# A two-layer decoder trunk: the attention's head pairs as one pipeline, with 64-row scores and w_o's first two groups by turns

## The chip, the core and the metric

The kernel runs on one NeuronCore of a Trainium2 chip: TensorE (PE, with its weight loads PEld), VectorE (DVE), ScalarE (ACT), GpSimd (POOL) and SyncE (SP), each with its own queue of instructions, joined by semaphores. The metric is the device time of one launch in microseconds (us).

## What is computed

One sequence of 256 positions, width 2048, two layers: a recurrent layer (RG-LRU) with a SwiGLU FFN, then a shared K/V projection, an attention layer and a second FFN. The change is in the attention layer only:

```python
D_MODEL = 2048; SEQ = 256; HEAD_DIM = 64; N_HEADS = 32; N_KV_HEADS = 4; WINDOW = BLOCK = 128
...
def attn_block(x, g, w_q, q_g, sinks, w_o, k_band, v_band):
    h = rms_norm(x, g)
    q = rms_norm((h @ w_q).reshape(bsz, s, N_KV_HEADS, GROUP, HEAD_DIM), q_g)
    ...
    scores = jnp.einsum("bnqhgd,bnkhd->bnhgqk", q, k_band) * (1.0 / math.sqrt(HEAD_DIM))
    scores = jnp.where(mask, scores, NEG_INF)
    ...                                   # one learned sink logit per head joins the softmax
    probs = jax.nn.softmax(jnp.concatenate([scores, sink], axis=-1), axis=-1)[..., :-1]
    out = jnp.einsum("bnhgqk,bnkhd->bnqhgd", probs, v_band)
    return x + out.reshape(bsz, s, N_HEADS * HEAD_DIM) @ w_o
```

Queries of block 0 see the 128 keys of their own block, queries of block 1 the 256 keys of both.

## The kernel before

Features lie on the 128 partitions and the 256 positions (`T`) along the free dimension. Every big product is a sum of three: weights and activations are split into a rounded high part and a rest (`hi`, `lo` of the weights; the two halves of a slot `s` of the activations), and high x high, high x rest and rest x high are added in PSUM. `group` makes one group of 512 output features: four PSUM banks, one for each tile `f` of 128 features, and `nk // 2` steps (jobs) of two input tiles each. Each step is one 512 KB weight load on SP's queue, one split on ACT (L242) and DVE (L243), and 24 matmuls of 256 columns at L280. In the steps that `SYNC` names, (0, 2, 5), three times two of them are merged to one of 512 columns ("h" in `products`), in a row. Such a bank then holds two halves, which the drain adds (`two`).

`stream` runs all steps in order. Attention, norms and splits of activations are background tasks (generators), stepped once or more at each half step (`half_tick`, `run_bg`), where their matmuls are put between the products. Counters of estimated DVE and ACT time (`self.dve`, `self.act`, `pe`) limit how many steps are taken. Tile's scheduler then sets the final order on each engine's queue, and may put a background matmul some rows later than the code has it. At most `MISC` = 4 of the 8 banks are lent to background tasks.

Attention has 16 pairs of heads (128 features each). Each group of w_q brings four pairs and a task that computes their norm (L910) and starts one `head_pair` per pair. A pair's four stages:

- scores (L799 to L801): K stands in `kd`, two slots (high and rest), each with the head's 64 features on partitions 0 to 63 for the first head and 64 to 127 for the second, zeros elsewhere, so that one matmul over 128 rows gives both heads: for block 0 three of 256 columns, for block 1 three of 512;
- softmax on DVE (L813 adds the mask and takes the maximum, then `ts`) and ACT (Exp);
- transposes (L847), six of 128 x 128, three to a bank, which ACT copies to two slots;
- values (L866 to L868): per head three fp32 matmuls of 64 output rows, the two heads in the two column halves of the array; then the split to `at[k]`, an input tile of w_o.

Pairs run beside each other as far as banks and slots allow. `project` with w_o has four groups of eight steps, in each of which step c waits for `at[2c]` and `at[2c+1]`; `residual` adds the result to x and prepares the next norm.

Of the kernel before, what the change touches and what calls it, by code (L numbers as in the profile page):

```python
# [48 lines left out]
class Trunk:  # L49
# [5 lines left out]
    NORM = 6  # L55
    MISC = 4
# [215 lines left out]
    def products(self, todo, ps, hi, lo, x2, begun, last):  # L272


        for n, (k, f, p) in enumerate(todo):
            if 2 * n in (len(todo), len(todo) + 1):
                self.half_tick()
            high, c0, c1 = self.PARTS[p]
            w = (hi if high else lo)[:, k * 512 + f * P:k * 512 + f * P + P]
            self.nc.tensor.matmul(ps[f][:, 0:c1 - c0], w, x2[k][:, c0:c1], start=f not in begun,  # L280
                                  stop=last and all(q[1] != f for q in todo[n + 1:]))
            begun.add(f)

    def group(self, src, nk, xs, done, last=False, sync=()):


        st = {}
        both = [(k, f) for k in range(2) for f in range(4)]
        for c in range(nk // 2):
            def mm(hi, lo, c=c):  # L290
                if c == 0:
                    st["ps"] = [self.bank() for _ in range(4)]
# [15 lines left out]
                self.products(todo, st["ps"], hi, lo, x2, st["begun"], c == nk // 2 - 1)  # L308
                if last:
                    for q in x2:  # L310
                        self.free(q)
                if c == nk // 2 - 1:
                    done([(p, bool(sync) and f < 2) for f, p in enumerate(st["ps"])])
            self.jobs.append((src(c), mm))

    def pull(self, bank, o=None, r=None):

        ps, two = bank
# [11 lines left out]
        self.free_bank(ps)  # L330
        return o
# [65 lines left out]
    def residual(self, g, ps, gains, r, out=None):  # L397
        for f in range(4):
            xt = self.x[g][:, f, :]
            p, two = ps[f]  # L400
# [5 lines left out]
            self.free_bank(p)  # L406
            if out is not None:
                self.nc.sync.dma_start(out[:, 4 * g + f, :], xt)
# [10 lines left out]
    def project(self, w, nk, xs, gains, r, out=None):  # L419
        for g in range(4):  # L420
            def done(ps, g=g):
                self.residual(g, ps, gains, r, out)
            self.group(lambda c, g=g: w[g, c], nk, xs, done, g == 3, () if out is not None and g == 3 else self.SYNC)
# [233 lines left out]
    def kv(self, xs, r, gains):  # L657
# [7 lines left out]
        def done(ps):  # L665
            k0 = [self.pull((p, False)) for p in ps[:2]]
# [4 lines left out]
            def task():  # L671
# [31 lines left out]
                for h in range(4):  # L703
# [21 lines left out]
        for c in range(8):  # L725
            def mm(hi, lo, c=c):
                if c == 0:
# [3 lines left out]
                    for h in range(4):  # L731
                        self.kd[h].ap = [self.slot() for _ in range(2)]
                        self.kvs += self.kd[h].ap
                        for q in self.kd[h].ap:
                            self.dve += 280
                            nc.vector.memset(q[0:64, T:2 * T].bitcast(F32), 0.0)
                            nc.vector.memset(q[64:P, 0:T].bitcast(F32), 0.0)
# [35 lines left out]
    def attn(self, xs, r, gains, rn):  # L773
# [4 lines left out]
        self.pairs = 0  # L778
# [4 lines left out]
        def head_pair(k, qs, rr):  # L783

            while not (self.kd[k // 4].ready and self.v[0].ready and self.v[1].ready):
                yield 1
            kd, f = self.kd[k // 4].ap, k % 4
            sm = self.half()
            mx, nm, es, den = (sm[:, 4 * i:4 * i + 4] for i in range(4))
            ps, sc = [], []  # L790
            for b in range(2):
                while not self.room():
                    yield 1
                p = self.mbank()
                n = P * (b + 1)
                o = p[:, 0:2 * n].rearrange("p (h n) -> p h n", h=2)
                kh, kl = (q.rearrange("p (h n) -> p h n", h=2)[:, :, 0:n] for q in kd)
                qh, ql = (qs[:, i * T + b * P:i * T + b * P + P] for i in range(2))
                nc.tensor.matmul(o, qh, kh, start=True, stop=False)  # L799
                nc.tensor.matmul(o, qh, kl, start=False, stop=False)  # L800
                nc.tensor.matmul(o, ql, kh, start=False, stop=True)  # L801
                ps.append(p)
                self.pe(330 * (b + 1))
            yield 1
            for hh in range(2):
                while not self.slots:
                    yield 1
                s = self.slot(F32)
                sc.append(s)
                for b, c0, c1 in blocks:  # L810
# [3 lines left out]
                        s[:, c0:c1], ps[b][:, hh * (c1 - c0):(hh + 1) * (c1 - c0)], con[:, K_MASK + c0:K_MASK + c1],  # L814
                        rr[:, b * 8 + f * 2 + hh:b * 8 + f * 2 + hh + 1],
                        par[:, C_SINK + 4 * k + hh:C_SINK + 4 * k + hh + 1], ALU.add, ALU.max,
                        accum_out=mx[:, i:i + 1])
                yield
            for p in ps:
                self.free_mbank(p)  # L820
            self.free(qs)
# [18 lines left out]
            yield 1  # L840
            ps, pT = [], []
            for hh in range(2):
                while not self.room():
                    yield 1
                p = self.mbank()
                for j in range(3):
                    nc.tensor.transpose(p[:, j * P:(j + 1) * P], sc[hh][:, j * P:(j + 1) * P], one)  # L847
                ps.append(p)
                self.pe(400)
            yield 1  # L850
            for hh in range(2):
                s = self.slot(F32)
                pT.append(s)
                self.a(s[:, 0:384], ps[hh][:, 0:384])
                self.free_mbank(ps[hh])
                self.free(sc[hh])
                yield
            yield 1
            while not self.room():
                yield 1  # L860
            p = self.mbank()
            c = (k // 4) * HD
            v0, v1 = (q.ap[:, c:c + HD] for q in self.v)
            for hh in range(2):
                o, t = p[64 * hh:64 * hh + 64, :], pT[hh]
                nc.tensor.matmul(o[:, 0:P], v0, t[:, 0:P], start=True, stop=True)  # L866
                nc.tensor.matmul(o[:, P:T], v0, t[:, P:T], start=True, stop=False)  # L867
                nc.tensor.matmul(o[:, P:T], v1, t[:, T:3 * P], start=False, stop=True)  # L868
                self.free(t)
                self.pe(400)  # L870
            yield 1
            s = self.slot()
            self.split_act(s, p[:, 0:T])
            self.free_mbank(p)
            at[k].ap = s
            at[k].ready = True
            self.pairs += 1
            if self.pairs == ND:
                for q in self.kvs:
                    self.free(q)  # L880
            yield

        for g in range(4):
            def done(ps, g=g):
# [6 lines left out]
                def task():  # L891
# [21 lines left out]
                    rr, m, t = (self.rrs[g % 2][:, 16 * i:16 * i + 16] for i in range(3))  # L913
# [11 lines left out]
                    for f in range(4):  # L925
                        self.spawn(head_pair(4 * g + f, qs[f], rr))
                        yield 2
                self.spawn(task())
            self.group(lambda c, g=g: w[g, c], ND, xs, done, g == 3, self.SYNC)
        self.project(self.d["w_o"], ND, at, gains, rn)  # L930


    def run(self):
# [5 lines left out]
        self.rrs = [const.tile([P, 48], F32, name=f"rr{i}") for i in range(2)]  # L939
# [85 lines left out]
```

## Time and profile before

| | before |
|---|---|
| median of 3 runs | 1997.57 us (1997.15 to 2000.5) |
| profiled execution, device time | 1996.68 us |
| its span in the trace | 1994.9 us |
| TensorE clock granted | 1.00 |
| q1 (all weight loads) | 373.60 MB, 58.3% of 16 DMA engines |

A row of the timeline has start, length, engine, line, operation, out<-in, rows*columns of the array in use, the moving operand's size and the count of instructions merged in it. In `out<-in` the moving operand comes first, then the weights: `b` is a PSUM bank, `s` a slot, `con` constants. The ends of matmuls are modelled, so the distance of two starts tells what one costs. An fp32 matmul appears as two instructions. In the rows of windows come the busy times of PE, PEld, DVE, ACT and POOL, then the clock, DMA's share and GB/s.

### The profile page before, as it was taken

How to read it: one execution, taken by the hardware profiler on the slowest of the kernel's cores; microseconds unless marked ns; L12 is line 12 of the kernel's file. 1: busy time of each engine (PE TensorE's matmuls, PEld its weight loads, DVE VectorE, ACT ScalarE, POOL GpSimd, SP SyncE). 2: the span in 40 equal slices, each digit the busy share in tenths (PEclk: the TensorE clock that was granted, in tenths of full speed). 3: DMA queues.
4: the chain of work that ended last, by engine and by line, in shares of the span. 5: the costliest groups of instructions: out<-in, count | busy, mean ns of one | idle time of the engine just before them, and what ended most of it. 6: DMA issues, size and time to landing. Idle time of an engine off the chain costs nothing.

```text
span 1994.9 us, 40283 instructions
## 1 busy us (share of the span) xinstructions
PE 1986.6 (100%) x16793; PEld 1953.1 (98%) x16793; DVE 1283.6 (64%) x2067; ACT 1079.3 (54%) x1627; POOL 0.2 (0%) x4
## 2 busy tenths in 40 slices
PE   9999999999999999999999999999999999999999
PEld 8999999999999999999999999999999999999999
DVE  8989866556556655545768786765565566554543
ACT  7798755445445444444556775554454454444342
POOL 0000000000000000000000000000000000000000
PEclk9999999999999999999999999999999999999999
DMA  7655655665666655565654335666666656656664
GB/s 267 201 183 173 216 191 192 197 194 191 196 195 191 197 194 192 194 197 191 194 187 146 119 117 169 192 190 194 197 191 193 196 192 193 197 192 204 206 204 128
DMA packets 105015, 376.58 MB, mean 189 GB/s; under 512 B 11648, under 2 KB 13824, under 8 KB 104832
## 3 DMA queue, kind: packets, MB, share of 16 engines
q1 hardware_dynamic: 104544, 373.60, 58.3%
q8 instruction: 131, 2.15, 0.4%
q14 instruction: 52, 0.43, 0.1%
q10 hardware_dynamic: 288, 0.40, 0.1%
HBM read 371.86 MB, written 2.10 MB: 187 GB/s over the span
## 4 chain that ended last, share of the span: by engine, by line
PE 98%; ACT 1%; DMA 0%; DVE 0%; issue 0%; SPq 0%; DVEq 0%; ACTq 0%
PE b L280 93%; PE b L559 1%; PE b L847 1%; PE b L755 1%; DMA x<-in_x 0%; PE b L910 0%; PE b L866 0%; PE b L799 0%; PE b L801 0%; PE b L800 0%; PE b L868 0%; PE b L867 0%; ACT hi L242 0%; PE b L764 0%; PE b L765 0%
## 5 line engine op out<-in xcount | busy, mean ns | idle before, releaser
L280 PE MATMUL b<-s,hi 128*128 128x256 f32 (+1 forms) x10406 | 1427.0, 283 | 3.7 <-ACT s L106 1.8
L280 PEld LDWEIGHTS b<-s,hi 128*128 128x128 f32 x10406 | 1318.7, 188 | 31.8 <-ACT hi L242 2.5
L243 DVE TENSOR_TENSOR lo<-raw,hi 128x1024 fp32r<-128x1024 f32 (+1 forms) x705 | 860.9, 1222 | 660.7 <-ACT hi L242 657.0
L242 ACT ACTIVATE hi<-raw 128x1024 fp32r<-128x1024 f32 (+1 forms) x705 | 745.7, 1059 | 770.4 <-PE b L280 740.9
L280 PE MATMUL b<-s,lo 128*128 128x256 f32 x5504 | 823.0, 277 | 0.0
L280 PEld LDWEIGHTS b<-s,lo 128*128 128x128 f32 x5504 | 715.1, 188 | 0.0
L106 ACT ACTIVATE t<-b 128x256 f32<-128x256 f32 x134 | 50.4, 385 | 62.2 <-PE b L280 37.8
L106 ACT ACTIVATE h<-h 128x256 f32<-128x256 f32 (+1 forms) x104 | 38.9, 376 | 21.0 <-DVE h L115 21.0
L106 ACT ACTIVATE s<-h 128x256 fp32r<-128x256 f32 (+1 forms) x106 | 42.7, 412 | 12.3 <-DVE h L115 9.8
L106 ACT ACTIVATE s<-s 128x256 f32<-128x256 f32 (+1 forms) x112 | 41.2, 415 | 5.1 <-DVE s L119 4.6
L115 DVE TENSOR_TENSOR h<-b,rstd 128x256 f32<-128x256 f32 x100 | 41.0, 416 | 0.0
L106 ACT ACT_TABLE_LOAD x31 | 39.8, 1283 | 0.5
L115 DVE TENSOR_TENSOR h<-h,rstd 128x256 f32<-128x256 f32 x94 | 39.1, 420 | 1.5
L106 ACT ACTIVATE s<-x,par 128x256 fp32r<-128x256 f32 x80 | 37.9, 498 | 2.6 <-DVE x L115 1.8
L115 DVE TENSOR_TENSOR h<-b,t 128x256 f32<-128x256 f32 x92 | 38.2, 418 | 0.0
L115 DVE TENSOR_TENSOR s<-s,s 128x256 fp32r<-128x256 f32 (+1 forms) x80 | 31.2, 420 | 9.6 <-ACT s L106 9.5
L119 DVE SCALAR_TENSOR_TENSOR s<-x,par,s 128x256 fp32r<-128x256 f32 x80 | 36.7, 479 | 0.5 <-ACT s L106 0.5
L115 DVE TENSOR_TENSOR s<-h,s 128x256 fp32r<-128x256 f32 x88 | 36.6, 418 | 0.0
L115 DVE TENSOR_TENSOR h<-h,h 128x256 f32<-128x256 f32 x88 | 36.5, 416 | 0.0
L106 ACT ACTIVATE s<-b 128x384 f32<-128x384 f32 (+3 forms) x68 | 28.0, 431 | 10.2 <-PE b L868 5.6
L106 ACT ACTIVATE s<-s,h 128x128 f32<-128x128 f32 x64 | 28.3, 444 | 6.2 <-DVE h L124 6.2
L115 DVE TENSOR_TENSOR x<-x,b 128x256 f32<-128x256 f32 x64 | 25.2, 415 | 8.9 <-PE b L280 8.9
(103 smaller groups left out, 618.8 us busy)
## 6 DMA issues: line engine op xcount, KB each, us to landing
raw<-in_ffn_in SPq DMA_DIRECT2D x352, 512.0 KB, 3.9
raw<-in_ffn_out SPq DMA_DIRECT2D x176, 512.0 KB, 3.5
raw<-in_lru_in SPq DMA_DIRECT2D x63, 512.0 KB, 4.0
raw<-in_lru_out SPq DMA_DIRECT2D x32, 512.0 KB, 3.4
raw<-in_w_q SPq DMA_DIRECT2D x32, 512.0 KB, 3.4
raw<-in_w_o SPq DMA_DIRECT2D x32, 512.0 KB, 3.7
raw<-in_gate SPq DMA_DIRECT2D x8, 512.0 KB, 3.7
raw<-in_kv SPq DMA_DIRECT2D x8, 512.0 KB, 3.3
```

The source lines that it names most:

```text
L106: self.nc.scalar.activation(out, in_, func, **kw)
L115: self.nc.vector.tensor_tensor(out, a, b, op)
L119: self.nc.vector.scalar_tensor_tensor(out, a, s, b, op0, op1)
L242: self.nc.scalar.activation(hi[:, q], raw[:, q], AF.Copy)
L243: self.nc.vector.tensor_tensor(lo[:, q], raw[:, q], hi[:, q].bitcast(F32), ALU.subtract)
L280: self.nc.tensor.matmul(ps[f][:, 0:c1 - c0], w, x2[k][:, c0:c1], start=f not in begun, stop=last and all(q[1] != f for q in todo[n + 1:]))
L559: nc.tensor.matmul(out[j], (hi if high else lo)[:, c:c + P], x2[kt][:, q:q + T], start=kt == 0 and high > q, stop=kt == 1 and not high)
L755: nc.tensor.matmul(ps[f][:, 0:T], w0, x2[kt][:, q:q + T], start=k0 + kt == 0 and high > q, stop=k0 + kt == ND - 1 and not high)
L847: nc.tensor.transpose(p[:, j * P:(j + 1) * P], sc[hh][:, j * P:(j + 1) * P], one)
```

## The change

`head_pair` is replaced by one task, `pairs`, that visits three pairs at a time: the values of the oldest, the transposes of the next and the scores of a new one are issued together, then the copies and the softmax. Visits are at least `VISIT` = 3 half steps apart. `kd` becomes one slot per head group, with K in both partition halves and without zeros; each head's scores are matmuls over 64 rows (partitions 0 to 63, or 64 to 127), into a bank of its own. The transposes fill one and a half banks instead of two, and the values use the free half. The values of a head are one matmul of 256 columns and one of 128 instead of three of 128, and the two heads alternate.

w_o's first two groups keep two tiles in a bank (`paired`), two banks each, without the merged 512-column products, and their steps go by turns: six of the first, six of the second, two of the first, two of the second.

```diff
+    VISIT = 3
...
-    def group(self, src, nk, xs, done, last=False, sync=()):
+    def group(self, src, nk, xs, done, last=False, sync=(), paired=False, jobs=None):
...
+                    if paired:
+                        ps = [self.bank() for _ in range(2)]
+                        st["ps"] = [(ps[f // 2][:, f % 2 * T:f % 2 * T + T], False, f // 2, f % 2) for f in range(4)]
+                        st["bank"] = ps
...
-    def project(self, w, nk, xs, gains, r, out=None):
+    def project(self, w, nk, xs, gains, r, out=None, late=0):
+        first = [[], []]
...
+            if late and g < 2:
+                self.group(src, nk, xs, done, paired=True, jobs=first[g])
+                if g:
+                    n = nk // 2 - late
+                    self.jobs += first[0][:n] + first[1][:n] + first[0][n:] + first[1][n:]
...
-                    kh, kl = self.kd[h].ap
-                    for i in range(2):
-                        q, c = slice(64 * i, 64 * i + 64), slice(i * T, i * T + T)
-                        self.a(kh[q, c], p[q, 0:T])
-                        self.tt(kl[q, c], p[q, 0:T], kh[q, c].bitcast(F32), ALU.subtract)
+                    self.split_act(self.kd[h].ap, p[:, 0:T])
...
+        def values(k, pT, p):
+            c = (k // 4) * HD
+            v0, v1 = (q.ap[:, c:c + HD] for q in self.v)
+            o = [p[HD * hh:HD * hh + HD, T:2 * T] for hh in range(2)]
+            for hh in range(2):
+                nc.tensor.matmul(o[hh], v0, pT[0][:, hh * T:(hh + 1) * T], start=True, stop=False)
+            for hh in range(2):
+                nc.tensor.matmul(o[hh][:, P:T], v1, pT[1][:, hh * P:(hh + 1) * P], start=False, stop=True)
...
+        def transposes(sc, ps):
+            for hh in (1, 0):
+                for j in (2, 1, 0):
+                    o = ps[0][:, hh * T + j * P:hh * T + j * P + P] if j < 2 else ps[1][:, hh * P:hh * P + P]
+                    nc.tensor.transpose(o, sc[hh][:, j * P:(j + 1) * P], one)
...
+        def scores(k, qs, ps):
+            kd = self.kd[k // 4].ap
+            for b, c0, c1 in blocks:
+                for i, j in ((1, 0), (0, 0), (0, 1)):
+                    for hh in range(2):
+                        q = slice(HD * hh, HD * hh + HD)
+                        nc.tensor.matmul(ps[hh][:, c0:c1], qs[q, i * T + b * P:i * T + b * P + P],
+                                         kd[q, j * T:j * T + c1 - c0], start=i == 1, stop=j == 1)
...
+        def pairs():
+            A = B = None
...
+                if A:
+                    values(A[0], A[1], pt[1])
+                    self.pe(900)
+                if B:
+                    transposes(B[1], pt)
+                    self.pe(700)
+                if new:
+                    scores(new[0], new[1], ps)
+                    self.pe(900)
+                yield 1
...                      # ACT copies B's transposes, splits A's values; then the new pair's softmax
+                yield max(1, at_tick + self.VISIT - self.tick)
...
-        self.project(self.d["w_o"], ND, at, gains, rn)
+        self.project(self.d["w_o"], ND, at, gains, rn, late=2)
```

PE's queue at the third pair's scores, before (matmuls by line, tile and size; 799 to 801 scores, 847 transposes of the next older pair, 866 to 868 values, 280 products):

```order
L799 MATMUL b_84<-s_11066,s_11676 128x256
L800 MATMUL b_84<-s_11067,s_11676 128x256
L801 MATMUL b_84<-s_11066,s_11676 128x256
L847 MATMUL b_89<-con,s_11840 128x128
L799 MATMUL b_88<-s_11066,s_11676 128x512
L847 MATMUL b_89<-con,s_11840 128x128 x2
L847 MATMUL b_87<-con,s_11843 128x128 x3
L800 MATMUL b_88<-s_11067,s_11676 128x512
L801 MATMUL b_88<-s_11066,s_11676 128x512
L280 MATMUL b_83<-s_11303,lo_80 128x256
L866 MATMUL b_89<-s_11871,s_11090 64x128
L867 MATMUL b_89<-s_11871,s_11090 64x128
```

The same visit now (804 and 806 values, 825 scores, 814 transposes, 281 products; the second and third pair of score rows, which read like the first, are left out):

```order
L804 MATMUL b_83<-s_11811,s_11072 64x256 x2
L806 MATMUL b_83<-s_11812,s_11072 64x128 x2
L825 MATMUL b_88<-s_11068,s_11649 128x128
L825 MATMUL b_89<-s_11068,s_11649 128x128
...
L825 MATMUL b_88<-s_11068,s_11649 128x256
L814 MATMUL b_83<-con,s_11816 128x128
L814 MATMUL b_86<-con,s_11816 128x128 x2
L814 MATMUL b_83<-con,s_11815 128x128
L814 MATMUL b_86<-con,s_11815 128x128 x2
L825 MATMUL b_89<-s_11068,s_11649 128x256
L825 MATMUL b_88<-s_11068,s_11649 128x256
L281 MATMUL b_85<-s_11243,hi_76 128x256 x2
```

The values moved ahead of the scores, the scores alternate between two banks, and the transposes, written ahead of the scores in `pairs`, stand behind the ninth of the twelve.

PE's queue where w_o's first group ends and the next begins, before (`b_83`, `b_87`, `b_85`: banks of the next group):

```order
L280 MATMUL b_88<-s_13307,lo_82 128x256
L280 MATMUL b_88<-s_13323,hi_78 128x256 x2
L280 MATMUL b_88<-s_13323,lo_82 128x256
L280 MATMUL b_83<-s_11967,hi_75 128x512
L280 MATMUL b_83<-s_11970,hi_75 128x512
L280 MATMUL b_87<-s_11967,hi_75 128x512
```

The place behind the last pair's values now (`b_84` and `b_86` the second group's banks, `b_85` and `b_90` the first's):

```order
L804 MATMUL b_87<-s_13452,s_11072 64x256 x2
L806 MATMUL b_87<-s_13453,s_11072 64x128 x2
L281 MATMUL b_86<-s_13067,hi_78 128x256 x4
L281 MATMUL b_84<-s_13003,lo_82 128x256 x2
...
L281 MATMUL b_85<-s_13291,hi_75 128x256 x4
L281 MATMUL b_90<-s_13291,hi_75 128x256 x4
```

Here the sixth step of the second group is followed by the seventh of the first, all in products of 256 columns; the first merged products of 512 columns stand where the third group begins.

More of the change, by code (lines that the diff above doesn't have):

```diff
@@ L270, with products @@
     PARTS = {"h": (1, 0, 2 * T), "a": (1, 0, T), "b": (1, T, 2 * T), "l": (0, 0, T)}
-    def products(self, todo, ps, hi, lo, x2, begun, last):
+    def products(self, todo, ps, hi, lo, x2, begun, last, paired=False):
         for n, (k, f, p) in enumerate(todo):
@@ L279, in products @@
             w = (hi if high else lo)[:, k * 512 + f * P:k * 512 + f * P + P]
-            self.nc.tensor.matmul(ps[f][:, 0:c1 - c0], w, x2[k][:, c0:c1], start=f not in begun,
-                                  stop=last and all(q[1] != f for q in todo[n + 1:]))
-            begun.add(f)
-    def group(self, src, nk, xs, done, last=False, sync=()):
+            self.nc.tensor.matmul(ps[f][0][:, 0:c1 - c0], w, x2[k][:, c0:c1], start=ps[f][2] not in begun,
+                                  stop=last and all(q[1] != f for q in todo[n + 1:]),
+                                  skip_group_check=paired)
+            begun.add(ps[f][2])
+    def group(self, src, nk, xs, done, last=False, sync=(), paired=False, jobs=None):
         st = {}
+        jobs = self.jobs if jobs is None else jobs
         both = [(k, f) for k in range(2) for f in range(4)]
@@ L731, in mm @@
                     for h in range(4):
[L732 to L737, printed above, removed]
+                        self.kd[h].ap = self.slot()
+                        self.kvs.append(self.kd[h].ap)
                     s = self.slot(F32)
@@ L777, in attn @@
         r2 = self.r2
-        self.pairs = 0
         one = con[:, K_ID:K_ID + P]
         blocks = ((0, 0, P), (1, P, 3 * P))
[L783 to L787, printed above, removed]
+        todo = deque()
+        def values(k, pT, p):
[6 more added lines that the diff above has]
+                nc.tensor.matmul(o[hh][:, P:T], v1, pT[1][:, hh * P:(hh + 1) * P], start=False, stop=True)
+            for q in pT:
+                self.free(q)
@@ L788, in head_pair, with softmax @@
+        def softmax(k, rr, ps, sc):
+            f = k % 4
             sm = self.half()
             mx, nm, es, den = (sm[:, 4 * i:4 * i + 4] for i in range(4))
[L790 to L803, printed above, removed]
@@ L858, in head_pair @@
-            yield 1
-            while not self.room():
-                yield 1
[L861 to L881, printed above, removed]
+        def pairs():
+            A = B = None
+            n = 0
+            while n < ND or A or B:
+                new = None
+                if todo and self.kd[todo[0][0] // 4].ready and self.v[0].ready and self.v[1].ready:
+                    new = todo.popleft()
+                    n += 1
+                elif not (A or B):
+                    yield 1
+                    continue
+                at_tick = self.tick
+                count = 2 * bool(A or B) + 2 * bool(new)
+                while self.misc + count > self.MISC or len(self.banks) < count or len(self.slots) < 5:
+                    yield 1
+                pt = [self.mbank() for _ in range(2)] if A or B else None
+                ps = [self.mbank() for _ in range(2)] if new else None
+                if A:
[7 more added lines that the diff above has]
+                    self.pe(900)
+                yield 1
+                nextA = None
+                if B:
+                    s = [self.slot(F32) for _ in range(2)]
+                    self.a(s[0], pt[0])
+                    self.a(s[1][:, 0:T], pt[1][:, 0:T])
+                    nextA = (B[0], s)
+                    yield
+                if A:
+                    s = self.slot()
+                    self.split_act(s, pt[1][:, T:2 * T])
+                    at[A[0]].ap = s
+                    at[A[0]].ready = True
+                    yield
+                for p in pt or ():
+                    self.free_mbank(p)
+                A, B = nextA, None
+                if new:
+                    sc = [self.slot(F32) for _ in range(2)]
+                    yield from softmax(new[0], new[2], ps, sc)
+                    B = (new[0], sc)
+                yield max(1, at_tick + self.VISIT - self.tick)
+            for q in self.kvs:
+                self.free(q)
@@ L938, in run @@
         self.r2 = const.tile([P, 2], F32, name="r2")
-        self.rrs = [const.tile([P, 48], F32, name=f"rr{i}") for i in range(2)]
+        self.rrs = [const.tile([P, 48], F32, name=f"rr{i}") for i in range(4)]
         self.rv = {i: Val() for i in range(4)}
```

66 lines of the change are left out of this document (27 added, 39 removed).

## The prediction

> **What bounds the kernel now.** I read the page first: span, busy shares, the chain that ended last.
>
> ```profile
> span 1994.9 us, 40283 instructions
> PE 1986.6 (100%) x16793; PEld 1953.1 (98%) x16793; DVE 1283.6 (64%) x2067; ACT 1079.3 (54%) x1627; POOL 0.2 (0%) x4
> PE 98%; ACT 1%; DMA 0%; DVE 0%; issue 0%; SPq 0%; DVEq 0%; ACTq 0%
> ```
>
> TensorE carries 98% of the chain. The waits of PE over the whole run are the second view (us in total, times, longest):
>
> ```profile
> PE b L280 <- ACT s L106: 1.8, 1, 1.8
> PE b L280 <- ACT hi L242: 1.8, 2, 1.5
> PE b L251 <- DVE lo L248: 1.2, 1, 1.2
> PE b L384 <- DVE acc L115: 0.4, 1, 0.4
> ```
>
> That is 5.2 us in all, and the same view cut to 1062 to 1225 us, where the attention runs, has no row for PE. So nothing can be won there by shorter waits. The time is what TensorE issues, at the spacing of its matmuls. Third, two stages side by side (PE, PEld, DVE, ACT busy, clock, DMA):
>
> ```profile
> 800.00:1000.00 200.00, 200.00 (x1740) 198.89 (x1738) 111.87 (x139) 93.35 (x116) 0.00 (x0) 1.00 0.59 194
> 1062.00:1203.00 141.00, 141.00 (x1169) 133.04 (x1168) 111.21 (x370) 108.49 (x287) 0.00 (x0) 1.00 0.37 120
> ```
>
> In the attention stage DMA moves 120 GB/s against 194: the weights wait for TensorE. DVE is busy 79% there, ACT 77%; neither ends the chain. Clock 1.00 in both. So the sum below counts starts of matmuls in PE's timeline (start, length, engine, line). "Busy" is no use, since ends overlap.
>
> **Spacing of the big matmuls.** A 256-column product has two paces:
>
> ```profile
> 603.78 1.07 PE L280 MATMUL b<-s,lo 128*128 128x256 f32 x8
> 604.69 1.52 PE L280 MATMUL b<-s,hi 128*128 128x256 f32 x12
> ...
> 1207.74 1.10 PE L280 MATMUL b<-s,lo 128*128 128x256 f32 x8
> 1208.68 2.05 PE L280 MATMUL b<-s,hi 128*128 128x256 f32 x16
> ...
> 1219.98 2.00 PE L280 MATMUL b<-s,hi 128*128 128x256 f32 x13
> 1221.83 1.07 PE L280 MATMUL b<-s,lo 128*128 128x256 f32 x8
> 1222.73 1.52 PE L280 MATMUL b<-s,hi 128*128 128x256 f32 x12
> ```
>
> 0.91/8 = 0.113 us in the long stages, 0.94/8 = 0.1175 after a disturbance. The step back to 0.113 comes at 1219.98, in the row of 13 which holds the three 512-column "h" products of `SYNC`.
>
> **Scores.** One pair before, six matmuls, three of 256 and three of 512 columns:
>
> ```profile
> 1073.93 0.28 PE L799 MATMUL b<-s,s 128*128 128x256 f32 x1
> ...
> 1074.75 0.39 PE L801 MATMUL b<-s,s 128*128 128x512 f32 x1
> 1074.98 2.05 PE L280 MATMUL b<-s,hi 128*128 128x256 f32 x16
> ```
>
> 1.05 us a pair, 16.8 us for 16, and no loss at either edge. The change makes 12 of them, six on rows 0 to 63 and six on rows 64 to 127, three of 128 and three of 256 columns on each. What one costs is not in this trace; the nearest rows bound it. From below: sixteen matmuls with 128 weight columns that move 2 columns each,
>
> ```profile
> 1070.96 1.84 PE L910 MATMUL b<-con,s 128*128 128x2 f32 x16
> 1072.67 0.48 PE L280 MATMUL b<-s,hi 128*128 128x256 f32 x2
> ```
>
> take 1.71 us, 0.107 each: loading 128 weight columns sets that, however little moves. So a half-array score with 128 weight columns is not below 0.107, and I take 0.117 for 128 and 256 columns alike (the row of the same number format). If the two halves run beside each other a pair takes 6 x 0.117 = 0.70, in all 11.2: a gain of 5.6 us. If they run one after the other it is 1.40, a loss of 5.6.
> The Trainium skill (TensorE: Matmul & The Clock Gate, "LDWEIGHTS (loading the stationary operand)") says that the load goes by columns and not by rows; by that half the rows save no load time, and the 0.107 agrees for whole rows. By that rule the sum stands as below; if half the rows loaded in half the time, the three narrow scores could take 0.06 and the sum would be 16 x 3 x 0.057 = 2.7 us lower.
>
> **Values.** One pair before, between big products:
>
> ```profile
> 1098.03 1.80 PE L280 MATMUL b<-s,hi 128*128 128x512 f32 x11
> 1099.76 0.43 PE L866 MATMUL b<-s,s 128*64 128x128 f32 x2
> 1100.03 0.27 PE L867 MATMUL b<-s,s 128*64 128x128 f32 x1
> 1100.03 0.32 PE L866 MATMUL b<-s,s 128*64 128x128 f32 x1
> ...
> 1100.52 0.38 PE L868 MATMUL b<-s,s 128*64 128x128 f32 x2
> 1100.83 0.50 PE L280 MATMUL b<-s,hi 128*128 128x256 f32 x2
> 1101.18 1.10 PE L280 MATMUL b<-s,lo 128*128 128x256 f32 x8
> ```
>
> Each fp32 matmul is two passes (12 rows for 6 in the code), 0.11 apart within a head; the second head's first pass (the second 1100.03) starts when the first head is at its third. The two 64-column halves of the array therefore do run together, the second 0.27 us late. The block reaches from 1099.68 (8 products of 256 and 3 of 512 columns after 1098.03 at 0.1175 and 0.235) to 1101.18 - 2 x 0.1175 = 1100.945: 1.27 us. In it the first pass starts 0.08 late and takes 0.16, not 0.11: 0.14 to enter. From the last pass's end (1100.63 + 0.11) to 1100.945 is 0.20 to leave. Work: 0.93. Two pairs back to back:
>
> ```profile
> 1086.72 0.28 PE L280 MATMUL b<-s,lo 128*128 128x256 f32 x1
> 1086.92 0.43 PE L866 MATMUL b<-s,s 128*64 128x128 f32 x2
> ...
> 1088.34 0.38 PE L868 MATMUL b<-s,s 128*64 128x128 f32 x2
> 1088.65 0.39 PE L799 MATMUL b<-s,s 128*128 128x256 f32 x1
> 1088.88 0.28 PE L800 MATMUL b<-s,s 128*128 128x256 f32 x1
> ```
>
> From 1086.84 to 1088.88 - 0.12 = 1088.76: 1.92, less 0.34 for the edges 1.58. In PE's order of before, counted over the program, there are four such doubles and eight singles: work 4 x 1.58 + 8 x 0.93 = 13.8 us. After the change the heads alternate (`values`), so both start at once: per head two passes of 256 and two of 128 columns, 6 x 0.109 = 0.65; 16 x 0.65 = 10.4. Gain 3.4 us.
>
> **Transposes** are the same 96, 0.109 apart, and only the edge differs:
>
> ```profile
> 1096.53 0.38 PE L868 MATMUL b<-s,s 128*64 128x128 f32 x2
> 1096.84 0.88 PE L847 MATMUL b<-con,s 128*128 128x128 f32 x6
> 1097.47 0.36 PE L280 MATMUL b<-s,lo 128*128 128x256 f32 x1
> 1097.67 0.40 PE L280 MATMUL b<-s,hi 128*128 128x256 f32 x2
> ```
>
> Values end at 1096.64 + 0.11; the six transposes end at 1097.67 - 0.12. That is 0.80 for 0.65 of work: 0.15 to switch into a transpose from the half-column mode; none from transposes into products.
>
> **Switches, the price of the change.** Before, only the values leave the full-array mode: 12 entries at 0.14, 8 exits at 0.20, 4 exits into transposes at 0.15, 3.9 us. Now the scores have a half-array mode of their own. The order of the whole program has 69 switches: 16 into values, 8 into transposes, 45 others. In 7 of the visits the transposes stand inside the scores, not ahead of them as `pairs` writes it, which makes two switches more. No row shows a switch into half the rows. From below it costs nothing (transposes and products alternate at their own spacing in rows 1097.47 and 1097.67), from above what the half-column mode pays. I take the latter: these too are half-array shapes, with 128 columns to load as on the exit, 0.20. 16 x 0.14 + 8 x 0.15 + 45 x 0.20 = 12.4 us, 8.5 more. With no cost for row halves, only the values' edges stay, 16 x 0.34 = 5.4: then it is 1.5 more.
> The Trainium skill (TensorEngine Tiling (Array Packing), "Key Properties") says that changing the tiling mode, not just the tile, drains TensorE. It speaks against this change; the exit of 0.20 agrees for columns, and no run here shows it for rows. By it the switches are 8.5 us more, without it 1.5.
>
> **w_o.** The two paired groups issue the same products and the same 64 loads on SP's queue, in another order; no load goes past another tensor's. POOL does nothing. Six "h" triples go (18 products of 512 columns become 36 of 256, the same 0.23 us a pair), and with them the chances to get back to 0.113. Before, it was regained in step 5 of the second group (1219.98). Now the next triple stands in step 0 of the third, 3 steps x 24 x 0.1175 = 8.5 us later, or it takes until that group's step 5, 22.6 us. At 0.0042/0.113 = 3.7% that is 0.3 to 0.8; I take 0.8, since short quick stretches inside the first group go as well. The sixteen steps in turns keep PE supplied where the last pairs come later; it did not wait there before, so nothing is gained. The residual work of two groups falls due in two steps instead of ten; the 16 steps of the last two groups hide it on DVE (64%). If they did not, the FFN's first step would wait.
>
> **DVE and ACT** do the same softmax and copies; the memsets and half of kd's splits go, worth nothing on the path since PE covers them.
>
> **The sum**, against the profiled execution (1996.68): scores -5.6, values -3.4, switches +8.5, pace +0.8 = +0.3, hence 1997.0. The median of the runs shown is 0.9 above that execution: 1998.0, rounded to half a us. What counts as "same" is 0.2%, 4 us, about what a measurement of this kernel can tell.
>
> **Rivals.**
> *Faster: row halves need no switch.* For it: nothing drains where only the number format changes. Against it: the 0.14 and 0.20 of the only half-array shape that is here. Price -7.0: 1991.0. Chance 0.17.
> *Slower: the two row halves take turns*, in `scores`. For it: 0.107 for a weight load that moves 2 columns; if loads of both halves share one path, 12 x 0.117. Against it: two loads and passes at 1100.03 in different column halves, side by side. Price 16 x 0.70 = +11.2: 2009. It decides the sign once over a third of the overlap is lost (4 of 11 us). Chance 0.14.
> *Narrow scores are dear.* This format is never run here below 256 columns. At the fp32 price, two passes of 0.109, each pair gains 3 x 0.10 = 0.30: +4.8, 2003. Chance 0.11.
> *TensorE waits for the softmax.* Rows of one pair before (its last score, the scaling, the transpose):
>
> ```profile
> 1089.83 0.40 PE L801 MATMUL b<-s,s 128*128 128x512 f32 x1
> 1092.56 1.00 DVE L124 TENSOR_SCALAR s<-s,h 128x128 f32<-128x128 f32 x4
> 1093.60 0.27 PE L847 MATMUL b<-con,s 128*128 128x128 f32 x1
> ```
>
> The transpose follows the last scaling by 0.04 us: its place in the queue is exact to the row. The scores that it then stands in have three or more matmuls behind it, and all of w_q behind those; 0.3 us late in each of 16 visits is +5: 2003. Against it: 3.4 us are enough here, and a visit now leaves 36 products, 4.2 us, plus its values. Chance 0.08.
>
> **Numbers.** The forecast, no change: chance 0.50, its own range 1995 to 2001.5, which leaves 0.05 of it below and 0.03 above the 4 us. Faster: 0.17 + 0.05 = 0.22. Slower: 0.14, 0.08 of the narrow scores, 0.05 of the waits and 0.03: 0.30. Same: 0.48. The range reaches to the rival without switches (1991.0, half a us of spread) and to the narrow scores (2003); the turns lie outside.
>
> **What would show it.** Scores of one head pair: starts about 0.06 apart in two banks, 0.70 a pair (right), or 0.117 apart (turns). First product after scores 0.20 late. Values 0.65 between the edges. Transposes waiting for DVE would be rows in PE's waits, which were none. The pace stays 0.1175 until the third w_o group. The forecast fails if a half-row switch costs other than 0.14 to 0.20, or if the halves do not overlap.

## The result: 2008.72 us, slower by 0.53%

| | before | after |
|---|---|---|
| median, 4 runs each | 1997.36 us (1996.63 to 2000.5) | 2008.72 us (2007.98 to 2008.96) |
| ratio, 95% interval | | 1.0053 [1.0036, 1.0071] |
| profiled execution, span | 1996.68, 1994.9 us | 2007.98, 2006.2 us |

The forecast was 1998.0 with a range up to about 2003.5; the measured time lies above it, and the span grew by 11.3 us. In the runs shown here the kernel before takes either about 1996.5 or about 2000.0 us; the profiles put this down to the pace of its first layer, not to attention (last section), so the experiments are read by their rows and waits as much as by their medians.

The page of after, first part, and the engine line of its chain:

```profile
span 2006.2 us, 40340 instructions
PE 1988.6 (99%) x16843; PEld 1948.9 (97%) x16843; DVE 1275.2 (64%) x2043; ACT 1075.3 (54%) x1619; POOL 0.2 (0%) x4
PE 41%; DVE 1%; ACT 0%; issue 0%
```

PE's busy time grew by 2.0 us (1986.6 to 1988.6) in a span that is 11.3 us longer, so most of the loss is not work on PE. The chain is followed back over less than half the span here, so its shares can't be set against those of before. PE's waits name the place (us in total, times, longest):

```profile
PE b L814 <- DVE s L125: 9.7, 11, 1.0
PE b L281 <- ACT s L107: 1.9, 1, 1.9
PE b L281 <- ACT hi L243: 1.5, 1, 1.5
PE b L252 <- DVE lo L249: 1.2, 1, 1.2
PE b L396 <- DVE acc L116: 0.3, 1, 0.3
```

The last four sum to 4.9 and were there before (5.2). The first is new: 11 of the 16 sets of transposes (L814) wait 0.88 us each for the scaling that ends the softmax (L125). PE's timeline at the first visits:

```profile
1071.16 0.95 PE L825 MATMUL b<-s,s 64*128 64x128 f32 x12
1072.05 2.15 PE L281 MATMUL b<-s,hi 128*128 128x256 f32 x13
1074.03 1.10 PE L281 MATMUL b<-s,lo 128*128 128x256 f32 x8
1074.97 1.57 PE L281 MATMUL b<-s,hi 128*128 128x256 f32 x12
1076.47 0.95 PE L825 MATMUL b<-s,s 64*128 64x128 f32 x12
1077.36 0.74 PE L281 MATMUL b<-s,hi 128*128 128x256 f32 x4
1077.93 1.10 PE L281 MATMUL b<-s,lo 128*128 128x256 f32 x8
1078.88 0.75 PE L281 MATMUL b<-s,hi 128*128 128x256 f32 x5
1080.60 0.88 PE L814 MATMUL b<-con,s 128*128 128x128 f32 x6 [0.98 <-DVE s L125]
1081.23 1.54 PE L281 MATMUL b<-s,hi 128*128 128x256 f32 x11
...
1084.45 0.83 PE L825 MATMUL b<-s,s 64*128 64x128 f32 x9
1086.05 0.88 PE L814 MATMUL b<-con,s 128*128 128x128 f32 x6 [0.78 <-DVE s L125]
1086.86 0.50 PE L825 MATMUL b<-s,s 64*128 64x256 f32 x3
```

The five products of 1078.88 are through by 1079.5. PE then stands for a microsecond, with eleven products behind the transposes in its queue (1081.23) whose row shows no wait. At 1086.05 the waiting transposes hold up three scores as well. DVE in the same stretch:

```profile
1079.54 1.00 DVE L125 TENSOR_SCALAR s<-s,h 128x128 f32<-128x128 f32 x4
...
1084.58 0.16 DVE L116 TENSOR_TENSOR h<-h 128x4 f32<-128x4 f32 x1 [1.96 <-ACT s L107]
1084.78 0.18 DVE L131 RECIPROCAL h<-h 128x4 f32<-128x4 f32 x1
1084.99 1.01 DVE L125 TENSOR_SCALAR s<-s,h 128x128 f32<-128x128 f32 x4
```

Both scalings end 0.05 us ahead of the transposes (1080.54, 1086.00). So the first pair's chain of DVE and ACT took from 1072.1, where its scores ended, to 1080.5: 8.4 us. Between its scores and its transposes PE's queue holds 50 products, three of them of 512 columns, and the 12 scores of the next pair: 53 x 0.1175 + 1.1 = 7.3 us of work. The 1.1 us between is the wait (0.98 as shown).

### The profile page after: what moved, and what is told of

Its sections match the earlier page's. It is cut to its first block, busy times and chain, and to the rows that moved or that the text cites. A ratio compares the mean times of both kernels' runs of the same rounds, so it can differ in the third digit from the quotient of the medians.

```text
span 2006.2 us, 40340 instructions
## 1 busy us (share of the span) xinstructions
PE 1988.6 (99%) x16843; PEld 1948.9 (97%) x16843; DVE 1275.2 (64%) x2043; ACT 1075.3 (54%) x1619; POOL 0.2 (0%) x4
## 5 line engine op out<-in xcount | busy, mean ns | idle before, releaser
L107 ACT ACTIVATE s<-b 128x256 f32<-128x256 f32 (+2 forms) x64 | 24.7, 435 | 23.0 <-PE b L814 16.7
L837 DVE CUSTOM_DVE_ANT_0 s<-b,con,par 128x128 f32<-128x128 f32 x64 | 27.8, 472 | 6.3 <-PE b L825 6.1
```

The lines of the kernel that those rows point to most:

```text
L107: self.nc.scalar.activation(out, in_, func, **kw)
L837: nc.vector.tensor_tensor_reduce(sc[hh][:, c0:c1], ps[hh][:, c0:c1], con[:, K_MASK + c0:K_MASK + c1], rr[:, b * 8 + f * 2 + hh:b * 8 + f * ...
```

## Experiments

Two theories. The expectations name them by letters.

**P, the plan.** The order on PE's queue is set ahead of time by Tile's scheduler, here called the plan, which has prices of its own for each instruction. If it prices a 64-row matmul far above what the chip takes, it believes that twelve scores fill more of the softmax's time than they do, and puts the transposes too early. The chain itself would be fast enough.

**C, the chain.** Three pairs at once are too much for DVE and ACT, whose turnaround bounds each visit; the waits would then stay wherever the transposes are put.

Later runs ask which part of the change brings the waits.

**The transposes half a step later** (`e1_t_late`). In `pairs`:

```diff
-                if B:
-                    transposes(B[1], pt)
-                    self.pe(700)
                 if new:
                     scores(new[0], new[1], ps)
                     self.pe(900)
                 yield 1
+                if B:
+                    transposes(B[1], pt)
+                    self.pe(700)
+                    yield 1
```

> The transposes of a visit are issued half a step (12 products) after its scores instead of ahead of them; everything else as in the changed kernel. Theory P (place: in the changed kernel the transposes stand in PE's queue about 0.9 us before the softmax is done, and PE idles with products ready behind them): the waits of the transposes fall from 9.7 us to under 2.5, the seven splits of the scores go (7 x 0.4 = 2.8 us), so 2008.7 - 8 - 2.8 = about 1997, range 1995 to 2000. Rival C (chain: DVE and ACT cannot deliver a pair per visit, whatever the place): the waits stay at 7 us or more and the time at 2003 to 2007.

1998.91 us (11 runs), ratio 1.0006 [0.9997, 1.0015], span 1997.2. Waits, and a visit:

```profile
PE b L814 <- DVE s L125: 1.4, 2, 1.0
```
```profile
1093.72 0.65 PE L804 MATMUL b<-s,s 128*64 128x256 f32 x4
...
1094.52 0.96 PE L825 MATMUL b<-s,s 64*128 64x128 f32 x12
1095.40 0.51 PE L281 MATMUL b<-s,hi 128*128 128x256 f32 x2
...
1096.93 0.82 PE L814 MATMUL b<-con,s 128*128 128x128 f32 x6
```

Twelve products now lie between a visit's scores and its transposes. 9.7 us of waits became 1.4, and 9.0 us of the span came back, with the same DVE and ACT work per pair, as P had it. But the second and third pairs' scores also start further apart, 9.6 us (1076.96 and 1086.56) against 8.0 in after (1076.47 and 1084.45), so by itself this run leaves C a way out. The next one closes it.

**Scores over 128 rows in the changed pipeline** (`e2_rows128`). `kd` back to two zero-padded slots, six matmuls a pair as before; all else as changed.

```diff
-                    for hh in range(2):
-                        q = slice(HD * hh, HD * hh + HD)
-                        nc.tensor.matmul(ps[hh][:, c0:c1], qs[q, i * T + b * P:i * T + b * P + P],
-                                         kd[q, j * T:j * T + c1 - c0], start=i == 1, stop=j == 1)
...
+                kh, kl = (q.rearrange("p (h n) -> p h n", h=2)[:, :, 0:n] for q in kd)
...
+                nc.tensor.matmul(o, qh, kh, start=True, stop=False)
+                nc.tensor.matmul(o, qh, kl, start=False, stop=False)
+                nc.tensor.matmul(o, ql, kh, start=False, stop=True)
```

> The changed kernel's pipeline with the scores of before: 128 rows over a zero-padded kd, six matmuls a pair, no half-row mode. Theory P, with the cause that the planner prices the half-row matmuls as if they ran one after another (12 x 0.117 = 1.4 us where the chip takes 0.7): the waits of the transposes fall under 2.5 us, since the plan's and the chip's time for the scores agree again; pairs cost values 1.0 + scores 1.05 + transposes 0.66 = 2.7 us against 2.8 before, time 1996 to 1999. Rival C: the waits stay at 7 us or more, 2004 to 2008.

1999.24 us (10 runs), 1.0003 [0.9994, 1.0012]; the profiled execution has a span of 1999.0, with 3.2 us of the slower pace in the first layer.

```profile
PE b L822 <- DVE s L125: 0.2, 1, 0.2
```
```profile
1083.39 0.28 PE L834 MATMUL b<-s,s 128*128 128x256 f32 x1
...
1084.44 0.63 PE L281 MATMUL b<-s,hi 128*128 128x256 f32 x4
...
1088.38 0.82 PE L822 MATMUL b<-con,s 128*128 128x128 f32 x6
```
```profile
1086.45 1.01 DVE L125 TENSOR_SCALAR s<-s,h 128x128 f32<-128x128 f32 x4
```

The time is 0.24 us above P's range. A pair's scores take 1.05 us again, hardly less than the 1.08 that the twelve narrow ones take between products with their switches (worked out in the next section). The scaling shown is done 0.9 us ahead of its transposes, and the waits are gone, with three pairs a visit and the same chain. The second, third and fourth pairs' scores start 5.9 and 7.8 us apart, in after 8.0 and 8.1, so pairs follow each other faster than in after and still nothing waits. C falls. In the queue 67 products and 6 scores now lie between a pair's scores and its transposes, where 50 products and 12 scores lay. If the plan holds the same chain for as long in both, twelve narrow scores stand in it for 17 products and 6 wide scores: by the chip's 0.1175 and 1.05 us that is 3.0 us, 0.25 each. The first pairs of the other three w_q groups, counted alike, give 2.5, 1.6 and 1.6 us, 0.14 to 0.20 each. In after they take 0.06 each, and 0.09 with their switches. (A rough estimate, from counts of rows: what the plan reckons was not read out.)

**w_o by turns, alone** (`e3_turns_only`): the kernel before, with the new `group` and `project`.

```diff
-        self.project(self.d["w_o"], ND, at, gains, rn)
+        self.project(self.d["w_o"], ND, at, gains, rn, late=2)
```

> The kernel before with only w_o's first two groups paired and by turns. From the prediction's term: pace 0.1175 kept longer, +0.3 to +0.8 us, so 1997.5 to 1998.5, and the quick pace of 0.113 returns only in the third w_o group. Rival: the turns themselves cost or bring more (waits of PE in w_o, or pairs spread better), a change of over 3 us either way.

1998.66 us (10 runs), 1.0005 [0.9996, 1.0014], span 1996.7, 1.8 above. The products of 1040 to 1245 us lie 1.0 us further over 0.113 than before (4.3 against 3.3), and no wait is new. So the pace costs about the 0.8 us that was forecast for it; the other 0.8 us of the span was not traced.

**Visits further apart** (`e4_visit4`).

```diff
-    VISIT = 3
+    VISIT = 4
```

> The changed kernel with visits at least 4 half steps apart instead of 3. Theory P: 12 more products (1.4 us) lie between a pair's scores and its transposes, more than the 0.9 us of each wait, so the transposes' waits fall under 2.5 us; the splits of the scores mostly stay; the last pair comes later and w_o may wait for it once, 1 to 4 us: 1999 to 2003. Rival C: waits stay at 7 us or more and the time at 2007 or above.

2005.74 us (5 runs), 1.0034 [1.0021, 1.0047], span 2004.0, some 3 us of it the slower pace in the first layer.

```profile
PE b L814 <- DVE s L125: 4.5, 6, 1.3
```

A miss for both: the waits halve and don't go. With a half step more the final order puts eight of the 16 sets of transposes among the next pair's scores, where after has seven, so the distance in the code is partly taken back.

**A third of the scores** (`e5_third`): high x high alone, four 64-row matmuls a pair; the two correction terms of the scores are left out.

```diff
-                for i, j in ((1, 0), (0, 0), (0, 1)):
-                    for hh in range(2):
...
+                for hh in range(2):
+                    q = slice(HD * hh, HD * hh + HD)
+                    nc.tensor.matmul(ps[hh][:, c0:c1], qs[q, b * P:b * P + P],
+                                     kd[q, 0:c1 - c0], start=True, stop=True)
```

> The changed kernel with a third of its score matmuls: only high x high, four half-row matmuls a pair instead of twelve (the two correction terms are left out). Softmax, transposes, values and their order in the code stay. Theory P (the planner prices each half-row matmul too high and so sets the transposes too early in PE's queue): the transposes' waits fall with the number of these matmuls, from 9.7 us to under 2.5; in PE's order there are already 69 products between the first scores and the first transposes, where the changed kernel has 50. Scores take 0.23 + 0.4 for switches instead of 1.08, so 2008.7 - 8 - 16 x 0.45 = about 1993, 1990 to 1997. Rival C (DVE and ACT chain too slow for a pair per visit): the same softmax, TensorE earlier by 0.45 us a pair, so the waits grow to 10 us or more.

1989.14 us (one run), span 1987.4.

```profile
PE b L814 <- DVE s L125: 0.2, 1, 0.2
```

The scores that are left out are worth 16 x 0.46 = 7.4 us of work (a block to the first product 0.43 us instead of 0.89); the run is 18.8 us of span below after, so the waits went as well. The chain has the same work and less PE time to hide in, but now 69 products lie between the first pair's scores and its transposes. This is what P expects of a plan with fewer instructions to overprice, and C, which expected longer waits, fails here too. The time is 1 us below P's range.

**The other head first** (`e6_heads01`): the transposes begin with the head whose scaling comes first.

```diff
-            for hh in (1, 0):
-                for j in (2, 1, 0):
+            for hh in (0, 1):
+                for j in (0, 1, 2):
```

> The changed kernel with the transposes issued first head first (0, 1) and block by block, instead of second head first; the softmax scales the first head first. Rival H (the reversed order makes all six transposes wait for the last scaling): half of the 1.0 us of scaling is no longer waited for, the waits fall from 9.7 us to 5 or less, 2003 to 2005. Theory P: the planner sets the first transposes earlier by as much, and the waits stay near 9 us (7 to 12), time 2007 to 2011.

2007.57 us (one run).

```profile
PE b L814 <- DVE s L125: 5.9, 10, 1.0
```

The waits lie between what H and P had asked for (5 or less, 7 to 12); the time is in P's range. 3.8 us less of waits come with only 0.4 us less of span: the transposes now start earlier and are split by products and scores (84 changes between full array, half rows and half columns instead of 69; at some 0.2 us each that would be 3 us). The order within a set is no remedy.

**64-row scores, alone** (`e7_rows64_only`): the kernel before with its pairs beside each other, `kd` as one slot, scores as changed.

```diff
-                    kh, kl = self.kd[h].ap
...
+                    self.split_act(self.kd[h].ap, p[:, 0:T])
...
-                nc.tensor.matmul(o, qh, kh, start=True, stop=False)
-                nc.tensor.matmul(o, qh, kl, start=False, stop=False)
-                nc.tensor.matmul(o, ql, kh, start=False, stop=True)
...
+                    for hh in range(2):
+                        q = slice(HD * hh, HD * hh + HD)
+                        nc.tensor.matmul(ps[hh][:, c0:c1], qs[q, i * T + b * P:i * T + b * P + P],
+                                         kd[q, j * T:j * T + c1 - c0], start=i == 1, stop=j == 1)
```

> The kernel before with the 64-row scores alone (kd in one slot, a bank per head); pairs, values and w_o as before. Theory P: the chip's time for the scores hardly changes (0.70 + 2 x 0.20 for switches against 1.05, +0.8 us in all; a few switches more where transposes stand inside scores, up to 3 us), but the transposes are again set too early: waits of 4 to 10 us at the transposes, time 2001 to 2010. Rival V (the waits belong to the one-task pipeline with its visits, not to the 64-row scores): waits under 2 us, 1998 to 2000.

2010.46 us (4 runs), 1.0066 [1.0051, 1.0082], span 2006.3.

```profile
PE b L836 <- DVE s L124: 5.4, 8, 1.2
```

The narrow scores bring the loss without pipeline and turns, which rules out V. The waits are within what P expected, the median is 0.5 us above its range. 5.4 of the 11.4 us of span are the same wait. Counted from the starts of matmuls, scores with their switches cost about 3 us more than 16.8, and the values 1.9 more: their 192 passes are the same but lie 0.083 us apart on average instead of 0.073, since the two heads overlap less often. Why they do is open, and so are 1 to 2 us.

**Alternating values, alone** (`e8_values_alt`): the kernel before with

```diff
-                o, t = p[64 * hh:64 * hh + 64, :], pT[hh]
-                nc.tensor.matmul(o[:, 0:P], v0, t[:, 0:P], start=True, stop=True)
-                nc.tensor.matmul(o[:, P:T], v0, t[:, P:T], start=True, stop=False)
-                nc.tensor.matmul(o[:, P:T], v1, t[:, T:3 * P], start=False, stop=True)
...
+            o = [p[64 * hh:64 * hh + 64, 0:T] for hh in range(2)]
...
+            for hh in range(2):
+                nc.tensor.matmul(o[hh], v0, pT[hh][:, 0:T], start=True, stop=False)
+            for hh in range(2):
+                nc.tensor.matmul(o[hh][:, P:T], v1, pT[hh][:, T:3 * P], start=False, stop=True)
```

> The kernel before with the values alone changed: the two heads alternate, one fp32 matmul of 256 and one of 128 columns each. From the prediction's term: both column halves start at once, 0.27 us a block less, 12 blocks, so -3.3 us: about 1994 beside a before of 1997, no new switches and no waits. Rival: the heads' late start was hidden or a 256-column fp32 pass costs more than two of 128: within 1 us of before.

1995.95 us (11 runs), 0.9986 [0.9977, 0.9994]: the version that beats both. Its runs lie near 1993.2 and 1996.5, where those of the kernel before lie near 1996.6 and 2000.0: about 3.4 us in both.

```profile
1099.60 0.65 PE L866 MATMUL b<-s,s 128*64 128x256 f32 x4
1100.08 0.39 PE L868 MATMUL b<-s,s 128*64 128x128 f32 x4
1100.40 0.88 PE L847 MATMUL b<-con,s 128*128 128x128 f32 x6
```

Values to transposes 0.80 us, against 1.07 before (1095.77 to 1096.84).

**Without the turns**: `e9_t_late_noturns` is `e1_t_late`, and `e10_no_turns` is the changed kernel, both with

```diff
-        self.project(self.d["w_o"], ND, at, gains, rn, late=2)
+        self.project(self.d["w_o"], ND, at, gains, rn)
```

> The transposes half a step late, as in the first experiment, and w_o's four groups one after another as before (no turns). If the turns only cost (the experiment with the turns alone was about 1.8 us slower in span than before): 1998.9 - 1.8 = about 1997. If the pipeline needs them, since its last pairs come later: step 7 of w_o's first group waits for the last pairs, PE has no products ahead of the last values and transposes, and the time is 2000 to 2006 with waits of PE in w_o.

> The changed kernel without the turns: w_o's groups one after another. Theory P with turns that only cost: waits at the transposes near 9 us as in the changed kernel, 2007. If the pipeline needs the turns: the last four pairs' transposes and values find fewer products to run beside, waits of 12 us or more, 2010 to 2016.

2006.28 us (5 runs), 1.0037 [1.0023, 1.0051], and 2017.22 us (one run).

```profile
PE b L814 <- DVE s L125: 3.2, 4, 1.5
...
PE b L804 <- DVE s L116: 0.8, 1, 0.8
PE b L804 <- ACT s L107: 0.7, 1, 0.7
```
```profile
PE b L814 <- DVE s L125: 8.5, 10, 1.3
```

The first fence is of `e9_t_late_noturns`, the second of `e10_no_turns`. Both times are those of a pipeline that needs the turns, each just above its range; the waits at the transposes in `e10_no_turns` stay under the 12 us expected. Without the turns w_o's first group asks for the last pairs sooner, so less work stands between their stages and even the values wait: 5 us more of span than with the turns, and 9 in `e10_no_turns`, of which some 3 are the slower first layer. The turns cost 1 to 2 us alone and are worth more than that behind this pipeline.

## Why the prediction was wrong

**The step that failed** is the rival "TensorE waits for the softmax", held at 0.08 and +5 us: the forecast took it that the transposes would not wait, and they wait 9.7 us. Two things were wrong in the working. The place that the rival named was right.

First, its rows joined two pairs. "Rows of one pair" took the score at 1089.83 and the scaling at 1092.56, and so a chain of 3.4 us. But DVE was still at the maximum of that score's pair at 1091.83, and that pair's scaling is the next one:

```profile
1083.52 0.27 PE L847 MATMUL b<-con,s 128*128 128x128 f32 x1
...
1086.49 0.39 PE L801 MATMUL b<-s,s 128*128 128x512 f32 x1
```
```profile
1091.83 0.54 DVE L813 CUSTOM_DVE_ANT_0 s<-b,con,par 128x256 f32<-128x256 f32 x1
...
1092.56 1.00 DVE L124 TENSOR_SCALAR s<-s,h 128x128 f32<-128x128 f32 x4
...
1095.31 1.01 DVE L124 TENSOR_SCALAR s<-s,h 128x128 f32<-128x128 f32 x4
```

The scaling at 1092.56 belongs to the pair whose last score starts at 1086.49. From the end of that score (1086.88) to the transposes at 1093.60 are 6.7 us, not 3.4; for the first pair, from 1075.14 to 1083.52, it was 8.4, as it is in after. The argument "3.4 us are enough here, and a visit now leaves 36 products, 4.2 us" compared a chain that is half as long as the real one with a distance that isn't the one in the queue either.

Second, "exact to the row" was read as slack that stays exact. It is the work of a plan, and the row that the plan chose moved with the shape of the scores (`e2_rows128`, `e7_rows64_only`). That its prices for the narrow scores moved it is the reading that fits the counts; the prices themselves were not seen. The transposes wait 11 times, 0.88 us each, not 16 times 0.3. The order of after, shown ahead of the prediction, had the transposes inside the scores; multiplying out the 50 products and 12 scores ahead of the first set (7.3 us) against a chain of 8.4 would have given the sign.

**Scores, -5.6: right.** The halves run side by side: the first pass of the second head starts 3 to 4 ns after the first's, and a block between products (1076.47 above) costs 1.08 us in all: 0.09 to enter, 0.89 to the first product, 0.10 by which the second product is late. Work and switches had been put at 0.70 + 0.40. Narrow scores at the fp32 price and halves that take turns are both refuted.

**Switches, +8.5: right in size.** Entry and exit together cost 0.40 us a block for half the rows (1.08 less 0.68 of work), as the 0.20 + 0.20 taken from above, and not far from the 0.34 of half columns. The parts differ, 0.09 to enter and 0.31 for the rest against 0.14 and 0.20, so it is partly luck that the sum came out right. The Trainium skill (TensorEngine Tiling (Array Packing), "Key Properties") says that a change of mode drains TensorE; the 0.4 us a block agrees, for rows too. The rival without switches falls with it.

**Values, -3.4: right.** 3.4 in `e8_values_alt`.

**Pace, +0.8: right.** It is regained in w_o's third group, as said:

```profile
1239.46 2.00 PE L281 MATMUL b<-s,hi 128*128 128x512 f32 x13
1241.29 1.07 PE L281 MATMUL b<-s,lo 128*128 128x256 f32 x8
```

**The sum.** All of attention's blocks on PE (scores, transposes, values, their switches and waits) come to 45.4 us before and 55.8 after, added from starts. Less 9.7 of waits that is 46.1, 0.7 more than before, where the terms gave 0.5 less (45.0 before, 44.5 after). With 1.0 for the pace that makes +1.7 for what PE does, against the +0.3 forecast, and the waits are the rest of the 11.3. Without the waits the bundle still gains nothing: in `e2_rows128` the -3.4 of the values stands against 1.5 for more edges of the values (the prediction's own figure) and 1.8 for the turns, and less its slower first layer that run's span is 0.9 us above before. That nothing was gained "by shorter waits" was true; that none could arise was not looked at closely enough.

## What to carry to other kernels

Where a planner orders the queues, a change of an instruction's shape can move its neighbours, most of all if the planner misprices the new shape: take from the new order the instructions between a producer and its consumer, multiply them by spacings from the trace, and compare that with the length of the chain between them. Measure that chain for one and the same item, following it through every engine; the row that stands next to another in a pipelined loop is often of another item. Of several edits bundled in one change, time each alone: here one was worth 3.4 us and the bundle lost 11.

## What the runs showed of the hardware

The same kernel runs at two paces. In the kernel before, profiled at 1996.68 us, eight products of the first layer take 0.90 us; in `e8_values_alt`, profiled at 1997.25 us and the same code there, 0.94:

```profile
32.41 1.07 PE L280 MATMUL b<-s,lo 128*128 128x256 f32 x8
33.31 0.84 PE L280 MATMUL b<-s,hi 128*128 128x256 f32 x6
```
```profile
33.91 1.10 PE L280 MATMUL b<-s,lo 128*128 128x256 f32 x8
34.85 0.87 PE L280 MATMUL b<-s,hi 128*128 128x256 f32 x6
```

Over the first 330 us that adds up: products lie some 1 to 2 us in sum over 0.1133 in eight of the profiles, and 4.3 to 5.1 in four (`e2_rows128`, `e4_visit4`, `e8_values_alt`, `e10_no_turns`), at a granted clock of 0.998 to 1.00 in all twelve. That is about the step of 3.4 us between 1996.5 and 2000.0; no run of the kernel before at 2000.0 was profiled, so for that kernel it is inferred. A row of three 512-column products is where the quicker pace comes back in attention; what sets which one the first layer gets was not tried.
